# Convolution with a residual on one core: most of the weights' rows move from SyncE's queue to GpSimd's software queue

## The chip, the core and the metric

The kernel runs on one core of a Trainium2 chip. The metric is the device time of one execution in microseconds; lower is better. A core has five engines that work side by side, each with its own program: TensorE (PE, matrix products), VectorE (DVE), ScalarE (ACT), GpSimd (POOL) and SyncE (SP), which here only issues transfers. Transfers between the chip's memory (HBM) and the core's own memory (SBUF) are carried out by 16 DMA engines. A transfer can be issued by SyncE, or by GpSimd[...]. Engines wait for one another, and for transfers, through semaphores; a transfer adds 16 to its semaphore when it has landed.

## The reference

A 3x3 convolution with padding 1 over 16 images of 64 channels and 64x64 points, plus a residual, all in float32:

```python
batch, c_in, h, w, c_out, k = 16, 64, 64, 64, 64, 3
x_pad = np.pad(x, ((0, 0), (0, 0), (pad, pad), (pad, pad)), mode='constant')
output[b, co] += weight[co, ci, kh, kw] * x_pad[b, ci, kh:kh+h, kw:kw+w]   # summed over ci, kh, kw
return (output + residual).astype(np.float32)
```

x, the residual and the output are 16.8 MB each. The weights are 64 x 64 x 3 x 3 numbers, 147 KB.

## The kernel before

The images are taken in eight pairs; a pair fills the 128 partitions (2 images x 64 channels) with 4096 points each, 2 MB. The weights are read as 128 "half rows": for each output channel two rows of 32 input channels x 9 taps, 288 numbers or 1152 bytes.

All transfers go through SyncE's queue, in this order. The first pair's load is moved by a helper to the very front of the program, ahead of a barrier at which all engines meet at the start; everything after it is issued behind that barrier:

```python
    w_rows = weight.rearrange("co (h ci) kh kw -> (co h) (ci kh kw)", h=2)
    wraw = nc.alloc_sbuf_tensor("wraw", [128, 288], FP32)
    # ... cut
        for p in range(NPAIR):
            if p >= NXR:
                nc.sync.wait_ge(s_half, 2 * (p - NXR) + 3)      # a buffer of x is free again
            if p == 0:
                to_the_front(load_x(p))
                nc.sync.dma_start(out=wraw[:, :], in_=w_rows[:, :]).then_inc(s_w, 16)
            else:
                load_x(p)
            if p in (0, 1, 3, 5, 7):
                load_ro((p + 1) // 2)                            # residual, one or two pairs
        for k in range(NEARLY):                                  # three stores of two pairs
            nc.sync.wait_ge(s_add, 4 * k + 5)
            store(slice(2 * k, 2 * k + 2)).then_inc(s_out, 16)
    # ... cut; two stores of one pair follow at the end
```

GpSimd fills an identity matrix and zeroes some edges:

```python
        nc.gpsimd.memset(ident[:, :], 0.0).then_inc(s_id, 1)
        # ... cut: the diagonal, the edges of the four xp tiles, two blocks of wl
```

Before these lines GpSimd's program has four small memsets of constants, which stand ahead of the start-up barrier.

TensorE waits for the identity and the weights, transposes the weights in nine steps, and, once ScalarE and VectorE have copied them into bf16 blocks (wl), runs the convolution: 24 matrix products per image.

```python
        nc.tensor.wait_ge(s_id, NZERO)
        nc.tensor.wait_ge(s_w, 16)
        wraw3 = wraw.rearrange("p (ci t) -> p ci t", t=9)
        for t in range(9):
            i = nc.tensor.transpose(
                out=tp[0:32, t // 3, 128 * (t % 3) : 128 * (t % 3) + 128], in_=wraw3[:, :, t], identity=ident[:, :]
            )
```

ScalarE casts each image to bf16 (xp<-xr); VectorE adds TensorE's result to the residual in place (ro<-ps,ro), and ro is what is stored.

The helper that moves a transfer to the front takes the instruction out of the current block and puts it into the program's first block, ahead of the issuing engine's drain at the barrier:

```python
        at = next(
            i for i, e in enumerate(front) if e.engine == ins.engine and isinstance(e, mybir.InstDrain)
        )
        front.insert(at, copy.replace(ins, ...))
```

Of the kernel before, what the change touches and what calls it, by code (L numbers as in the profile page):

```python
# [15 lines left out]
def kernel(  # L16
# [7 lines left out]
    nc = tc.nc  # L24
# [20 lines left out]
    w_rows = weight.rearrange("co (h ci) kh kw -> (co h) (ci kh kw)", h=2)  # L45
# [9 lines left out]
    wraw = nc.alloc_sbuf_tensor("wraw", [128, 288], FP32)  # L55
# [1 line left out]
    ps = [psum.tile([128, NCHUNK, JC, W], FP32, name=f"ps{i}") for i in range(2)]  # L57

    sem = lambda name: tc.alloc_semaphore(name)
    s_w = sem("s_w")  # L60
    s_x = [sem(f"s_x{i}") for i in range(NXR)]
    s_r = [sem(f"s_r{i}") for i in range(2)]
    s_out = sem("s_out")
    s_id = sem("s_id")
    s_half = sem("s_half")
    s_pack = sem("s_pack")
    s_bank = sem("s_bank")
    s_conv = sem("s_conv")
    s_add = sem("s_add")

    def load_x(p):
        return nc.sync.dma_start(out=xr[p % NXR][:, :], in_=x_bc[128 * p : 128 * p + 128, :]).then_inc(s_x[p % NXR], 16)

    def load_ro(i):
        if i >= 2:
            nc.sync.wait_ge(s_r[i % 2], 16 * (i // 2))
        nc.sync.dma_start(out=ro[:, RES[i], :], in_=res_bc[:, RES[i], :]).then_inc(s_r[i % 2], 16)
# [24 lines left out]
    def to_the_front(dma):  # L102

        def fixed(ap):
            t = ap.bass_ap.tensor.name
            return mybir.PhysicalAccessPattern(
                ap=ap.ap, offset=ap.bass_ap.offset, dtype=ap.dtype, memref=t, memsetref=t + "_set", bass_ap=ap.bass_ap
            )  # L110

        front = nc.main_func.blocks[0].instructions
        here = nc.cur_bb.bb.instructions
        ins = here.pop()
        assert ins.name == dma.ins.name
        at = next(
            i for i, e in enumerate(front) if e.engine == ins.engine and isinstance(e, mybir.InstDrain)
        )
        front.insert(at, copy.replace(ins, ins=[fixed(a) for a in ins.ins], outs=[fixed(a) for a in ins.outs]))

# [4 lines left out]
    def weight_block(h, half, d, par, kh):  # L125

        at = 64 * half + 32 * h
        return dict(out=wl[at : at + 32, d, :, par, :], in_=tp[0:32, kh, 0:384].rearrange("p (kw co h) -> p kw co h", kw=3, h=2)[:, :, :, h])

    with tc.tile_critical(no_gpsimd_drain=True):  # L130

        for p in range(NPAIR):
            if p >= NXR:

                nc.sync.wait_ge(s_half, 2 * (p - NXR) + 3)
            if p == 0:
                to_the_front(load_x(p))
                nc.sync.dma_start(out=wraw[:, :], in_=w_rows[:, :]).then_inc(s_w, 16)
            else:
                load_x(p)  # L140
            if p in (0, 1, 3, 5, 7):
                load_ro((p + 1) // 2)
        for k in range(NEARLY):
            nc.sync.wait_ge(s_add, 4 * k + 5)
            store(slice(2 * k, 2 * k + 2)).then_inc(s_out, 16)


        nc.gpsimd.memset(ident[:, :], 0.0).then_inc(s_id, 1)  # L148
        nc.gpsimd.wait_ge(s_id, 1)
        nc.gpsimd.affine_select(  # L150
            out=ident[:, :],
            in_=ident[:, :],
# [14 lines left out]
        for n in range(B):  # L167
# [6 lines left out]
            i = nc.scalar.copy(out=t[64:128, 0:J, :], in_=x4[hp, :, 0, :])  # L174
# [4 lines left out]
            if n == 0:  # L179
                nc.scalar.wait_ge(s_id, NZERO + 1)  # L180
                for b in blocks[4:]:
                    for h in range(2):
                        i = nc.scalar.copy(**weight_block(h, *b))  # L183
# [4 lines left out]
        for k, b in enumerate(blocks[:4]):  # L188
            for h in range(2):
                i = nc.vector.tensor_copy(**weight_block(h, *b))  # L190
# [3 lines left out]
        for n in range(B):  # L194
# [4 lines left out]
            if im == 0:  # L199
                i = next(i for i, pairs in enumerate(RES) if p < pairs.stop)  # L200
                nc.vector.wait_ge(s_r[i % 2], 16 * (i // 2 + 1))
            for par in range(2):
                i = nc.vector.tensor_tensor(  # L203
                    out=o4[hp, :, par, :], in0=psj[64 * par : 64 * par + 64, :, :], in1=o4[hp, :, par, :], op=ADD
                )
# [4 lines left out]


        nc.tensor.wait_ge(s_id, NZERO)
        nc.tensor.wait_ge(s_w, 16)
        wraw3 = wraw.rearrange("p (ci t) -> p ci t", t=9)
        for t in range(9):
            i = nc.tensor.transpose(  # L216
                out=tp[0:32, t // 3, 128 * (t % 3) : 128 * (t % 3) + 128], in_=wraw3[:, :, t], identity=ident[:, :]
            )
# [23 lines left out]
        store(slice(p, p + 1))  # L242
    with tc.tile_critical(sync_engine=mybir.EngineType.Pool, no_gpsimd_drain=True):
        nc.gpsimd.wait_ge(s_out, 16 * NEARLY)
        tc.free_semaphores([s_w, *s_x, *s_r, s_out, s_id, s_half, s_pack, s_bank, s_conv, s_add])


# [28 lines left out]
```

## Time and profile before

| | before |
|---|---|
| device time, median of 3 (lowest to highest) | 122.76 us (122.69 to 122.91) |
| profiled execution: time, span | 122.68 us, 120.8 us |
| busy: PE, DVE, ACT, POOL | 87.9, 76.0, 63.1, 2.4 us |
| bytes moved, mean rate over the span | 50.48 MB, 418 GB/s |
| weights, from issue to landing | 7.1 us |
| first load of x, from issue to landing | 7.8 us |

The span runs from the first to the last instruction of the profiled execution, so it is shorter than the device time. A profile names a line of the kernel (L72), an engine, an operation and the tiles, output first. "SPq" stands for SyncE's sequencer, which issues transfers. A transfer's landing is counted from its issue and holds all its waiting behind others in the queue. The rates in the row of 40 slices are what all 16 DMA engines moved in each slice.

### The profile page before, as it was taken

What the parts mean: (1) busy time and instruction counts of PE and PEld (TensorE: products, weight loads), DVE (VectorE), ACT (ScalarE), POOL (GpSimd) and SP (SyncE); (2) the same over time, 40 slices, a digit from 0 to 9 for tenths busy, and PEclk for the clock granted to TensorE, in tenths of its full rate; (3) what the DMA queues carried; (4) which work ended last, traced back from release to release, by engine and by line L of the source; (5) the groups of instructions that cost most, each with busy time, mean ns of one, the idle gap of its engine ahead of it and who ended that gap; (6) DMA issues with size and microseconds to landing.
All of it is one profiled execution on the core that took longest, in us unless ns stands there. A gap on an engine that the chain in (4) does not pass through costs nothing.

```text
span 120.8 us, 734 instructions
## 1 busy us (share of the span) xinstructions
PE 87.9 (73%) x393; PEld 10.7 (9%) x105; DVE 76.0 (63%) x40; ACT 63.1 (52%) x37; POOL 2.4 (2%) x16
## 2 busy tenths in 40 slices
PE   0024499999999999999999999999999990000000
PEld 0011001101010011011111111011111100000000
DVE  0005400789898988989879898988989879500000
ACT  4049959948999923999960999883000000000000
POOL 5200000000000000000000000000000000000000
PEclk9999999999999999999999999999999999855555
DMA  7999999999999999999999999999999999999994
GB/s 168 428 428 428 428 428 434 428 434 434 428 434 434 434 428 434 434 434 434 434 434 423 423 428 434 423 412 434 434 434 434 423 434 434 434 428 434 434 434 174
DMA packets 3504, 50.48 MB, mean 418 GB/s; under 512 B 304, under 2 KB 432, under 8 KB 432
## 3 DMA queue, kind: packets, MB, share of 16 engines
q1 hardware_dynamic: 3504, 50.48, 98.5%
HBM read 33.70 MB, written 16.78 MB: 418 GB/s over the span
## 4 chain that ended last, share of the span: by engine, by line
PE 71%; DVEq 2%; DVE 2%; issue 0%
PE ps L87 53%; PE ps L86 18%; DVEq L130 2%; DVE ro L203 2%
## 5 line engine op out<-in xcount | busy, mean ns | idle before, releaser
L203 DVE TENSOR_TENSOR ro<-ps,ro 64x2048 f32<-64x2048 f32 x32 | 73.2, 2289 | 17.7 <-PE ps L87 17.2
L87 PE MATMUL ps<-xp,wl 128*128 128x504 bf16 (+1 forms) x288 | 80.0, 388 | 0.0
L86 PE MATMUL ps<-xp,wl 128*128 128x504 bf16 (+1 forms) x96 | 37.4, 389 | 3.4 <-PEq L224 3.4
L174 ACT CAST xp<-xr 64x2048 bf16<-64x2048 f32 x16 | 30.3, 1896 | 18.3 <-DMA xr<-in_x_dram 17.2
L178 ACT CAST xp<-xr 64x2048 bf16<-64x2048 f32 x16 | 30.4, 1897 | 0.4
L86 PEld LDWEIGHTS ps<-xp,wl 128*128 128x128 bf16 x96 | 9.5, 99 | 79.1 <-issue 79.1
L190 DVE CAST wl<-ps 32x192 bf16<-32x192 f32 x8 | 2.8, 348 | 10.6 <-PE ps L216 10.5
L216 PE MATMUL ps<-ident,wraw 128*32 128x128 f32 x9 | 2.1, 413 | 8.3 <-DMA wraw<-in_weight_dram 8.3
L216 PEld LDWEIGHTS ps<-ident,wraw 128*32 128x32 f32 x9 | 1.2, 137 | 8.7 <-issue 8.2
L174 ACT ACT_TABLE_LOAD x1 | 1.3, 1283 | 1.0 <-SPq L130 1.0
L183 ACT CAST wl<-ps 32x192 bf16<-32x192 f32 x4 | 1.2, 306 | 0.0
L162 POOL MEMSET xp<- 64x64 bf16 x4 | 0.6, 147 | 0.2
L161 POOL MEMSET xp<- 64x64 bf16 x4 | 0.6, 145 | 0.2
L150 POOL TENSOR_SCALAR_AFFINE_SELECT ident<-ident 128x128 f32<-128x128 f32 x1 | 0.3, 294 | 0.2 <-POOL ident L148 0.2
L164 POOL MEMSET wl<- 64x192 bf16 x1 | 0.3, 253 | 0.1
L163 POOL MEMSET wl<- 64x192 bf16 x1 | 0.3, 252 | 0.1
L148 POOL MEMSET ident<- 128x128 f32 x1 | 0.2, 205 | 0.6 <-SPq L130 0.6
L260 POOL MEMSET const-bfloat16-1.0<- 128x1 bf16 x1 | 0.1, 112 | 0.0
L260 POOL MEMSET const-uint8-127<- 128x1 uint8 x1 | 0.1, 112 | 0.0
L260 POOL MEMSET const-float32-0.0<- 128x1 f32 x1 | 0.1, 105 | 0.2 <-issue 0.2
L260 POOL MEMSET const-float32-1.0<- 128x1 f32 x1 | 0.1, 109 | 0.0
## 6 DMA issues: line engine op xcount, KB each, us to landing
xr<-in_x_dram SPq DMA_DIRECT2D x8, 2048.0 KB, 15.3
ro<-in_residual_dram SPq DMA_DIRECT2D x3, 4096.0 KB, 24.0
out_dram<-ro SPq DMA_DIRECT2D x3, 4096.0 KB, 33.2
ro<-in_residual_dram SPq DMA_DIRECT2D x2, 2048.0 KB, 15.9
out_dram<-ro SPq DMA_DIRECT2D x2, 2048.0 KB, 12.8
wraw<-in_weight_dram SPq DMA_DIRECT2D x1, 144.0 KB, 7.1
```

Of the source, the lines that this page charges most:

```text
L86: return e.matmul(out=out_, lhsT=lhsT, rhs=rhs, start=start, stop=stop, skip_group_check=True)
L87: return e.add_instruction(mybir.InstMatmult(name=nc.get_next_instruction_name(), engine=PE, ins=[e.lower_ap(rhs), e.lower_ap(lhsT)], outs ...
L130: with tc.tile_critical(no_gpsimd_drain=True):
L161: nc.gpsimd.memset(t[0:64, 0, :], 0.0).then_inc(s_id, 1)
L162: nc.gpsimd.memset(t[64:128, J, :], 0.0).then_inc(s_id, 1)
L174: i = nc.scalar.copy(out=t[64:128, 0:J, :], in_=x4[hp, :, 0, :])
L178: nc.scalar.copy(out=t[0:64, 1 : J + 1, :], in_=x4[hp, :, 1, :]).then_inc(s_pack, 1)
L183: i = nc.scalar.copy(**weight_block(h, *b))
L190: i = nc.vector.tensor_copy(**weight_block(h, *b))
L203: i = nc.vector.tensor_tensor(out=o4[hp, :, par, :], in0=psj[64 * par : 64 * par + 64, :, :], in1=o4[hp, :, par, :], op=ADD)
L216: i = nc.tensor.transpose(out=tp[0:32, t // 3, 128 * (t % 3) : 128 * (t % 3) + 128], in_=wraw3[:, :, t], identity=ident[:, :])
L260: nc = _bacc.Bacc("TRN2", target_bir_lowering=False, num_devices=1)
```

## The change

Of the weights' 128 half rows, the first 112 are now loaded by GpSimd's software queue. That transfer is put at the front of GpSimd's program, ahead of its constant memsets and so ahead of the start-up barrier, as the first load of x is on SyncE. The other 16 rows stay second on SyncE's queue. Each part has a semaphore of its own, and TensorE waits for both. The purpose is that most of the weights no longer stand behind the first load of x on one queue. The amount of data is the same; nothing else moves on TensorE, VectorE, ScalarE or SyncE.

```diff
-    s_w = sem("s_w")
+    s_w = [sem(f"s_w{i}") for i in range(2)]
...
+    def load_w(engine, rows, sem):
+        return engine.dma_start(out=wraw[rows, :], in_=w_rows[rows, :]).then_inc(sem, 16)
...
-            i for i, e in enumerate(front) if e.engine == ins.engine and isinstance(e, mybir.InstDrain)
+            i for i, e in enumerate(front) if e.engine == ins.engine and isinstance(e, (mybir.InstDrain, mybir.InstMemset))
...
-                nc.sync.dma_start(out=wraw[:, :], in_=w_rows[:, :]).then_inc(s_w, 16)
+                load_w(nc.sync, slice(112, 128), s_w[1])
...
+        to_the_front(load_w(nc.gpsimd, slice(0, 112), s_w[0]))
         nc.gpsimd.memset(ident[:, :], 0.0).then_inc(s_id, 1)
...
-        nc.tensor.wait_ge(s_w, 16)
+        for sem in s_w:
+            nc.tensor.wait_ge(sem, 16)
```

More of the change, by code (lines that the diff above doesn't have):

```diff
@@ L244 @@
         nc.gpsimd.wait_ge(s_out, 16 * NEARLY)
-        tc.free_semaphores([s_w, *s_x, *s_r, s_out, s_id, s_half, s_pack, s_bank, s_conv, s_add])
+        tc.free_semaphores([*s_w, *s_x, *s_r, s_out, s_id, s_half, s_pack, s_bank, s_conv, s_add])
 _INS = ['x', 'weight', 'residual']
```

## The prediction

> **What bounds the kernel now.** I read the chain that ended last first, since it names what the program seems to wait for, and then the page's row of slices and its queue table to see whether that chain is really the limit.
>
> ```profile
> span 120.8 us, 734 instructions
> PE 71%; DVEq 2%; DVE 2%; issue 0%
> PE ps L87 53%; PE ps L86 18%; DVEq L130 2%; DVE ro L203 2%
> ...
> GB/s 168 428 428 428 428 428 434 428 434 434 428 434 434 434 428 434 434 434 434 434 434 423 423 428 434 423 412 434 434 434 434 423 434 434 434 428 434 434 434 174
> q1 hardware_dynamic: 3504, 50.48, 98.5%
> HBM read 33.70 MB, written 16.78 MB: 418 GB/s over the span
> ```
>
> The chain names TensorE, but it covers only about 75% of the span; the rest of the time is after its last instruction. The row of slices says why: each slice is 120.8/40 = 3.02 us, and in 38 of 40 the transfers run at 412 to 434 GB/s. The one hardware queue fills 98.5% of sixteen engines' time. So the transfers are the bound. Only the first and last slices fall short, and the time can change only by the bytes in the queue, by the ramp at the start, or by a gap that opens in the queue.
>
> The windows view splits the start and the end (columns: stretch, length, then busy us of PE, PEld, DVE, ACT and POOL with counts, clock, mean DMA share, GB/s):
>
> ```profile
> 0.00:1.00 1.00, 0.00 (x0) 0.00 (x0) 0.00 (x0) 0.04 (x1) 0.22 (x5) 1.00 0.00 0
> 1.00:3.00 2.00, 0.00 (x0) 0.00 (x0) 0.00 (x0) 1.24 (x1) 1.39 (x9) 1.00 1.10 254
> 3.00:6.00 3.00, 0.00 (x0) 0.00 (x0) 0.00 (x0) 0.00 (x0) 0.78 (x4) 1.00 1.01 431
> 6.00:8.00 2.00, 0.00 (x0) 0.00 (x0) 0.00 (x0) 0.21 (x1) 0.00 (x0) 1.00 0.98 401
> ...
> 119.60:120.80 1.20, 0.00 (x0) 0.00 (x0) 0.00 (x0) 0.00 (x0) 0.00 (x0) 0.50 0.00 0
> ```
>
> Nothing moves for 1.0 us after the first issue. For the next 2 us the engines count as busy (share 1.10) but move only 254 GB/s: that is latency, not throughput. In the trace's packet records the first 16 KB packet of each engine takes 0.72 to 2.03 us, and a later one 0.611 us. The ramp therefore loses (431 - 254) x 2.0 us = 354 KB, or 354/431 = 0.82 us of full-rate work. The small dip to 401 GB/s at 6 to 8 us is where the weights' 128 packets of 1152 bytes pass: in the records each takes 51 ns and the next on the same engine starts 47 ns after it, so eight rows per engine take 8 x 47 = 0.38 us.
>
> The timeline shows who waits for those weights:
>
> ```profile
> 0.00 0.38 SPq L72 DMA_DIRECT2D xr<-in_x_dram  x1
> 1.00 0.33 SPq L138 DMA_DIRECT2D wraw<-in_weight_dram  x1
> 7.79 1.90 ACT L174 CAST xp<-xr 64x2048 bf16<-64x2048 f32 x1 [5.55 <-DMA xr<-in_x_dram]
> 8.27 2.08 PE L216 MATMUL ps<-ident,wraw 128*32 128x128 f32 x9 [8.27 <-DMA wraw<-in_weight_dram]
> 13.78 0.59 PE L86 MATMUL ps<-xp,wl 128*128 128x512 bf16 x1 [3.44 <-PEq L224]
> 99.67 4.61 DVE L203 TENSOR_TENSOR ro<-ps,ro 64x2048 f32<-64x2048 f32 x2 [0.58 <-PE ps L87]
> 104.58 0.98 SPq L80 DMA_DIRECT2D out_dram<-ro  x2
> ```
>
> The weights are second on SyncE's queue, so they land just behind the first image pair, and TensorE transposes them from 8.27 us. Its convolution then runs almost unbroken from 13.78 to 99.67 us. The last two stores are issued at 104.58 us, yet the packet records show the store ahead of them finishing at 109.9 us and the last one at 119.6 us. Allowing the 1.0 us from issue to first packet, compute could be about 109.4 - 104.6 - 1.0 = 3.8 us later before the queue ran dry (109.4 is when the first engine finishes that earlier store). An earlier convolution gains nothing.
>
> [...] The trace has 1.007 us from the issue to the first packet on SyncE's queue[...] and the software one is unseen. [...]
>
> **The change part by part.**
> Removed from SyncE's queue: 112 of 128 rows, 112 x 1152 = 129 KB. By the packet records that is seven packets per engine, 7 x 47 = 0.33 us; by bytes at 431 GB/s it is 0.30 us. This comes straight off the path, since SyncE's queue is the chain that really ends last.
>
> Added on GpSimd's queue: the same seven packets per engine and one completion packet (9 ns in the records for this kind). What they cost depends on when they run. GpSimd's first instruction in the trace starts at 0.23 us, the issue now stands ahead of it[...]. That falls in the ramp, which has 0.82 us of unused room against the 0.30 us needed. If they fit, the cost is only about 0.01 us; if they come after 3 us, they take 0.33 us from the first pair at full rate and the gain is nil.
>
> Moved on GpSimd: its four constant memsets, the start-up barrier behind them, the identity and the zero fills go back by however long GpSimd takes[...]. SyncE passes that barrier at about 1.0 us now. [...] the queue holds the first pair's packets until the first engine completes them at 6.44 us. So the barrier can slip by about 6.4 - 1.0 - 1.0 = 4.4 us before an engine idles. The fills end at 3.94 us and the transposes need them at about 8 us, again 4 us of room.
>
> Kept: 16 rows, one packet per engine, still behind the first pair. TensorE waits for both parts, so its start stays tied to that pair's end; it moves by at most 0.3 us either way, into the 3.8 us of slack, and counts for nothing. One more semaphore wait is too small to see.
>
> Sum: between -0.33 + 0.01 = -0.32 us (all rows in the ramp) and +0.01 us (none). I weight the full case above the empty one, since the issue is at the very front, and take -0.26 us: 122.76 - 0.26 = 122.50 us.
>
> **The rivals.**
> First, no gain because the ramp is not free. If the slow first packets are a shortage at the memory, and not a latency of each queue, added packets stretch them. For it: total rate in the ramp is low on all engines at once (254 GB/s). Against: the packets there look like waiting, with all sixteen engines showing long first packets and then 0.611 us at once. The time would stay at 122.7 to 122.9 us.
>
> Second, the software queue costs more than it saves: [...] some extra work at the program's start or end that comes with using it. The wait for the weights then moves from SyncE's queue to GpSimd's. As long as they land before about 11.5 us (3.8 us of slack past 7.8 us) only the lost packet time counts, and the result is 122.8 to 123.2 us.
>
> Third, GpSimd is held long enough to hold up the start-up barrier past its 4.4 us. [...] Against it: the issue was put at the front by design, and the memsets around it are ordinary GpSimd work that runs at once.
>
> A gain beyond 0.4 us has no source: even a perfect ramp, with the weights free, would leave 50.3 MB at about 431 GB/s on the queue.
>
> **Range and chances.** About half the weight is on 122.4 to 122.6 us, a quarter on no change near 122.8, the rest above. That gives 122.2 to 123.2 us for 8 times in 10. Two per cent is 2.46 us, so faster by that would need 120.3 us, which no step here can give: 0.01. Slower by that needs 125.2 us, the hard end of the third rival: 0.03. Within 2%: 0.96.
>
> **What would show it.** Right: a software queue with about 0.13 MB in the queue table; its 1152-byte packets starting before 3 us; the first slice's GB/s above 168; no dip at 6 to 8 us; first pair landing at about the same time; the whole run of transfers about 0.3 us shorter; the stores' backlog at the end still there. Wrong: the software rows starting after 3 us or landing after 8 us; SyncE's second issue later than about 5.4 us with a hole in the early slices; a GpSimd DMA taking several us; or a span that grows at the end, with the transfers over but the program not.

## The result, and the profile after

The changed kernel takes 126.25 us (median of 6 runs, 125.99 to 126.69), the kernel before 122.81 us in the same comparison: ratio 1.0283, 95% interval 1.0263 to 1.0302. It is 3.4 us slower. I had predicted 122.5 us, with a range of 122.2 to 123.2.

The page of the changed kernel, the lines that answer to those of before (its row of 40 slices is now 3.13 us to the slice):

```profile
span 125.4 us, 735 instructions
...
GB/s 172 421 116 199 429 434 434 423 439 429 429 439 434 423 439 423 434 439 429 429 423 439 429 434 434 434 402 434 423 418 439 434 439 439 423 418 434 434 434 125
...
q1 hardware_dynamic: 3392, 50.35, 95.4%
q0 software_dynamic: 48, 0.13, 0.3%
```

The software queue is there with its 0.13 MB, and takes 0.3% of the engines' time. The third and fourth slices have fallen to 116 and 199 GB/s, where before every slice but the first and last had over 400. So the queue ran dry for a time between 6 and 12 us. The windows view places it (same columns as in the prediction; the last is GB/s):

```profile
3.00:6.00 3.00, 0.00 (x0) 0.00 (x0) 0.00 (x0) 0.00 (x0) 0.00 (x0) 1.00 0.95 392
6.00:8.00 2.00, 0.00 (x0) 0.00 (x0) 0.00 (x0) 0.00 (x0) 0.00 (x0) 1.00 0.69 255
8.00:10.00 2.00, 0.00 (x0) 0.00 (x0) 0.00 (x0) 1.10 (x1) 0.71 (x4) 1.00 0.03 5
10.00:12.00 2.00, 0.07 (x1) 0.07 (x2) 0.00 (x0) 1.99 (x2) 1.44 (x9) 1.00 0.85 192
12.00:14.00 2.00, 2.00 (x9) 1.12 (x9) 0.00 (x0) 1.98 (x2) 0.00 (x0) 1.00 1.01 434
```

Between 8 and 10 us almost nothing moves, and from 10 to 12 us there is a second ramp at 192 GB/s. Over the first 14 us the engines average 249 GB/s against 372 in the kernel before; (372 - 249) x 14 us = 1.72 MB, and at 429 GB/s that is 4.0 us. The profiled span grew by 4.5 us (from 120.85 to 125.40 us in the trace), so nearly all of it is lost here; behind 14 us the mean rate is 426 against 429 GB/s. The timeline of the changed kernel shows who held the queue:

```profile
0.00 0.38 SPq L75 DMA_DIRECT2D xr<-in_x_dram  x1
0.75 0.65 POOL L72 DMA_DIRECT2D wraw<-in_weight_dram  x1 [0.75 <-issue]
1.44 0.10 POOL L265 MEMSET const-float32-0.0<- 128x1 f32 x1
1.54 0.10 POOL L265 MEMSET const-uint8-127<- 128x1 uint8 x1
8.90 1.28 ACT L178 ACT_TABLE_LOAD   x1 [8.90 <-SPq L133]
8.94 0.35 SPq L72 DMA_DIRECT2D wraw<-in_weight_dram  x1
8.94 0.20 POOL L152 MEMSET ident<- 128x128 f32 x1 [7.30 <-SPq L133]
17.44 0.58 PE L89 MATMUL ps<-xp,wl 128*128 128x512 bf16 x1 [3.40 <-PEq L229]
```

GpSimd's issue takes 0.65 us and its constant memsets are over at 1.64 us. Then no engine does any work until 8.90 us, when ScalarE, SyncE and GpSimd all start at once: the start-up barrier has opened, 7.9 us later than before. SyncE's second issue moves from 1.00 to 8.94 us. The transfers' landings say what came just ahead of that (KB, then us from issue to landing):

```profile
wraw<-in_weight_dram POOLq DMA_DIRECT2D x1, 126.0 KB, 7.7
wraw<-in_weight_dram SPq DMA_DIRECT2D x1, 18.0 KB, 1.7
```

The software rows were issued at 0.75 us and landed 7.7 us later, at 8.40 us; 0.5 us after that SyncE issued again. In the trace's packet records the first software packet starts only at 4.61 us and the last one ends at 7.92 us.

In the profiled runs device time minus span was 122.68 - 120.85 = 1.8 us before and is 126.69 - 125.40 = 1.3 us here, so the time grew 0.5 us less than the span. (126.69 us is the slowest of the six runs; hence 4.0 us in the profiled runs and 3.4 us in the medians.)

### The profile page after: what moved, and what is told of

It is laid out like the page before. It is cut to its first block, busy times and chain, and to the rows that moved or that the text cites. A ratio compares the mean times of both kernels' runs of the same rounds, so it can differ in the third digit from the quotient of the medians.

```text
span 125.4 us, 735 instructions
## 1 busy us (share of the span) xinstructions
PE 87.4 (70%) x393; PEld 10.7 (9%) x105; DVE 76.0 (61%) x40; ACT 63.2 (50%) x37; POOL 3.0 (2%) x17
## 5 line engine op out<-in xcount | busy, mean ns | idle before, releaser
L178 ACT CAST xp<-xr 64x2048 bf16<-64x2048 f32 x16 | 30.3, 1896 | 13.7 <-DMA xr<-in_x_dram 13.1
L72 POOL DMA_DIRECT2D wraw<-in_weight_dram x1 | 0.6, 646 | 0.7 <-issue 0.7
## 6 DMA issues: line engine op xcount, KB each, us to landing
out_dram<-ro SPq DMA_DIRECT2D x2, 2048.0 KB, 13.7
```

Of the source, the lines that this page charges most:

```text
L72: return engine.dma_start(out=wraw[rows, :], in_=w_rows[rows, :]).then_inc(sem, 16)
```

## The experiments

Theory A: GpSimd's program has a drain ahead of the start-up barrier, and this drain does not end until the software transfer issued ahead of it has landed; the barrier opens half a microsecond later, and by then SyncE's queue is empty. Theory B: GpSimd itself is held for a fixed time by the issue, and everything it does next waits. Theory C: the second queue slows the DMA engines, whatever the barrier does.

**The same issue, behind the drain.** Only the place in GpSimd's program differs from the changed kernel: behind the drain, still ahead of its wait at the barrier.

```diff
+        if ins.engine == mybir.EngineType.Pool:
+            at = 1 + next(i for i, e in enumerate(front) if e.engine == ins.engine and isinstance(e, mybir.InstDrain))
```

> The same software load of 112 rows, issued by GpSimd behind its drain instead of ahead of it, still before the start-up barrier is released. Theory A (GpSimd's drain ahead of the barrier does not end until the software transfer has landed, here 8.4 us, and the barrier opens some 0.5 us later): the barrier opens at about 1.0 us as in the kernel before, SyncE's second issue is at about 1.0 us, no hole in the transfers, time 122.5 to 123.0 us. Theory B (GpSimd itself is held[...], so everything it does next waits): either the barrier still opens at about 8.9 us and the time is about 126.2, or it opens early and GpSimd's identity memset starts only at about 8 us. Theory C (a second, software-fed queue slows the DMA engines): the time stays near 126 us although the barrier opens early.

Measured: 123.33 us (before in the same comparison: 122.89); ratio 1.0035, interval 1.0021 to 1.0049. Its timeline:

```profile
1.07 0.65 POOL L72 DMA_DIRECT2D wraw<-in_weight_dram  x1 [0.62 <-POOLq L267]
1.47 0.35 SPq L72 DMA_DIRECT2D wraw<-in_weight_dram  x1
1.72 0.22 POOL L154 MEMSET ident<- 128x128 f32 x1
9.19 2.08 PE L223 MATMUL ps<-ident,wraw 128*32 128x128 f32 x9 [9.19 <-DMA wraw<-in_weight_dram]
```

SyncE issues again at 1.47 us, and GpSimd fills its identity at 1.72 us, right after its issue ends, while the software rows are still 3 us from their first packet. So GpSimd was not held past its issue: theory B falls. Moving one issue past one drain takes back 3.0 of the 3.4 us. The time is still 0.44 us over before, 0.33 us above what A expected; that rest is taken up below.

**The same rows by ScalarE's hardware queue, at the front.**

```diff
-        to_the_front(load_w(nc.gpsimd, slice(0, 112), s_w[0]))
+        to_the_front(load_w(nc.scalar, slice(0, 112), s_w[0]))
```

> The same 112 rows at the front, issued by ScalarE on its hardware queue instead of GpSimd's software queue. Theory A (a software transfer under GpSimd's drain): with no software transfer the barrier opens at about 1.0 us; no hole; and if a second queue is served during the ramp the rows start before 2.5 us and the time is 122.4 to 122.7 us (the gain of up to 0.32 us that the prediction hoped for), or 122.7 to 122.9 us if the ramp is not free. If every drain waits for its engine's transfer, the barrier opens only when these rows land, at about 3 to 4 us, which is still early enough to leave no hole. Theory C for any second queue: near 126 us.

Measured: 122.93 us against 122.89; ratio 1.0007, interval 0.9996 to 1.0019. The barrier opens at about 1.1 us although the rows land at 8.4 us, so ScalarE's drain did not wait here for the transfer on its hardware queue (it lasts 0.15 us in the trace). A second queue costs nothing here, but gains nothing either. Windows of this kernel:

```profile
1.00:3.00 2.00, 0.00 (x0) 0.00 (x0) 0.00 (x0) 1.28 (x1) 1.32 (x8) 1.00 1.00 247
3.00:6.00 3.00, 0.00 (x0) 0.00 (x0) 0.00 (x0) 0.00 (x0) 0.84 (x5) 1.00 1.05 443
```

The ramp is as slow as before (247 against 254 GB/s): the rows' first packet starts at 2.98 us, when the ramp is about over, although the issue was at 0.12 us. From then on the rows take turns with x: sixteen of them, as many as there are DMA engines, start about every 0.67 us until 7.64 us, which is the time of one 16 KB packet of x (0.61 us) and one row (0.05 us).

**More work on SyncE's queue ahead of the held barrier.** The software load stays ahead of the drain; the second pair of x is issued ahead of the barrier too, and the 16 rows come by ScalarE's queue.

```diff
-                load_w(nc.sync, slice(112, 128), s_w[1])
+                load_w(nc.scalar, slice(112, 128), s_w[1])
+            elif p == 1:
+                to_the_front(load_x(p))
```

> The software load stays ahead of GpSimd's drain as in the changed kernel, but SyncE issues the second pair of x ahead of the barrier too, so that its queue holds 2 x 4.9 us of work; the 16 rows come by ScalarE's queue behind the barrier. Theory A and B (the loss is SyncE's queue running dry while the barrier is held): barrier still at about 8.5 to 9.5 us, no hole in the transfers until 12 us, time 122.5 to 123.2 us. Theory C (the software queue's own cost to the DMA engines): still 125 us or more.

Measured: 123.94 us (122.69 to 124.39) against 122.89; ratio 1.0069, interval 1.0048 to 1.0091. The barrier is held as in the changed kernel (SyncE's next issue at 8.86 us), yet no slice of its page but the first and last is under 363 GB/s: with more in the queue there is no hole, and most of the loss is gone. The median missed the expectation on the high side. In its packet records most 16 KB packets of the first two residual loads, from 12 to 24 us, take 0.700 us instead of 0.611 (218 of 256 to within 0.01 us); the x loads before and after them do not. That is 2 x 2.1 MB at 379 (14 to 23 us) instead of 431 GB/s, 1.3 us. The same stretch shows in the profiled run of the kernel with the issue behind the drain, for one residual load (0.7 us; this was its slowest run, 124.18 us). What causes it was not settled.

**Only 16 rows by the software queue.**

```diff
-                load_w(nc.sync, slice(112, 128), s_w[1])
+                load_w(nc.sync, slice(16, 128), s_w[1])
-        to_the_front(load_w(nc.gpsimd, slice(0, 112), s_w[0]))
+        to_the_front(load_w(nc.gpsimd, slice(0, 16), s_w[0]))
```

> Only 16 rows by the software queue, ahead of the drain as in the changed kernel; the other 112 second on SyncE's queue. Theory A with a fixed start-up of the software queue (its first packet came 3.9 us after its issue with 112 rows): the rows land at 5.5 to 7.5 us, the barrier opens 0.4 to 0.5 us after that, the hole is smaller, time 123.5 to 125.5 us. If the hold grows with the rows: landing near 2 us, no hole, 122.7 to 123.0 us. Theory B[...]: barrier at about 8.9 us as with 112 rows, time 126 us or more.

Measured: 125.23 us against 122.89; ratio 1.0184, interval 1.0169 to 1.0199. The rows land 6.1 us after their issue and SyncE issues again at 7.33 us: a seventh of the rows, and still four fifths of the hold (6.3 of 7.9 us). The first software packet starts at 4.99 us, as late as with 112 rows. Most of the delay is in when the software queue is first served, less in how much it carries: from the first packet to the landing it is 1.8 us with 16 rows and 3.8 us with 112.

**The software rows alone.** The first load of x is issued behind the barrier too.

```diff
-                to_the_front(load_x(p))
+                load_x(p)
```

> The changed kernel with the first load of x issued behind the barrier too, so that the software rows are alone on the DMA engines. Theory A (GpSimd's drain waits for the landing): the rows land earlier than the 8.4 us after the start that they took beside x, and the barrier opens 0.4 to 0.5 us after that landing, whenever it is; the first software packet tells the software queue's own start-up: if about 3.9 us after the issue again, it is the queue's, if about 1 to 2 us, it was the waiting behind x. Theory B (a fixed hold of GpSimd): the barrier still opens 8.1 us after the software issue. The time itself is expected at 126 to 129 us, since x starts only behind the barrier.

Measured: 125.61 us, one run, just under the expected 126 to 129 us. Timeline and landing of the rows:

```profile
0.75 0.65 POOL L72 DMA_DIRECT2D wraw<-in_weight_dram  x1 [0.75 <-issue]
3.70 0.38 SPq L75 DMA_DIRECT2D xr<-in_x_dram  x1
```

```profile
wraw<-in_weight_dram POOLq DMA_DIRECT2D x1, 126.0 KB, 2.4
```

The same transfer now lands at 3.17 us, and the barrier opens with it. Its first packet comes at 2.10 us, 1.35 us after the issue; beside the load of x it came 3.86 us after it. So alone the software queue takes 1.35 us to start, and the other 2.5 us came only with x's packets in flight; how they come about is not shown. The trace holds GpSimd's drain itself, as a record of its sequencer (here the kernel before, the changed kernel and this one; shortest, median and longest in ns, then first and last start in us):

```profile
L260 POOLq DRAIN  x1: 196/196/196, 0.3 to 0.3; - x1
L265 POOLq DRAIN  x1: 7658/7658/7658, 0.8 to 0.8; - x1
L265 POOLq DRAIN  x1: 2423/2423/2423, 0.8 to 0.8; - x1
```

The four kernels with a software issue ahead of the drain, from their records:

| kernel | rows landed at | drain ended at | SyncE's next issue |
|---|---|---|---|
| changed kernel | 8.40 us | 8.48 us | 8.94 us |
| more ahead | 8.33 us | 8.41 us | 8.86 us |
| 16 rows | 6.80 us | 6.88 us | 7.33 us |
| software alone | 3.17 us | 3.25 us | 3.70 us |

The landing varies by 5.2 us, and in all four the drain ends 0.08 us after it and SyncE issues 0.53 us after it: the barrier follows the landing, as theory A has it.

**The hold without the software queue.** The kernel before, with the barrier held by two long GpSimd memsets into buffers that are loaded later.

```diff
+        for i in (1, 2):
+            to_the_front(nc.gpsimd.memset(xr[i][:, :], 0.0))
         nc.gpsimd.memset(ident[:, :], 0.0).then_inc(s_id, 1)
```

> The kernel before, all weights on SyncE's queue, no software transfer; only the barrier is held, by two GpSimd memsets of 128 x 4096 ahead of the drain (estimate from the 128 x 128 memset's 205 ns against 105 to 112 ns for one element: 3.0 us each). Theory A (the cost is the held barrier and the queue running dry): the barrier opens at about 7 us, the transfers stop at about 7.5 to 8 us and start again 1.0 us after SyncE's second issue, and the time is 125.0 to 126.2 us. Theory C (the software queue itself is what costs): 122.7 to 123.2 us.

Measured: 126.12 us against 122.96; ratio 1.0250, interval 1.0227 to 1.0274. Timeline:

```profile
0.36 6.97 POOL L149 MEMSET xr<- 128x4096 f32 x2
7.79 1.28 ACT L176 ACT_TABLE_LOAD   x1 [7.79 <-SPq L130]
7.83 0.33 SPq L138 DMA_DIRECT2D wraw<-in_weight_dram  x1
```

A barrier that opens at 7.8 us costs 3.2 us with no software transfer in the program, as A expected. SyncE issues 1.1 us earlier than in the changed kernel, and the profiled span is 1.2 us shorter (124.2 against 125.4 us); in device time the 0.5 us noted with the result bring the two close together. The loss of the changed kernel needs nothing but the hold; theory C falls for its main part.

**The software rows behind the barrier**, as GpSimd's last instruction.

```diff
-        to_the_front(load_w(nc.gpsimd, slice(0, 112), s_w[0]))
...
         nc.gpsimd.memset(wl[64:128, 1, :, 0, :], 0.0).then_inc(s_id, 1)
+        load_w(nc.gpsimd, slice(0, 112), s_w[0])
```

> The software load of 112 rows as GpSimd's last instruction, behind the barrier and its fills, at about 4 us. Theory A: barrier at about 1.0 us, no hole, rows 3.9 us after their issue, landing at 9 to 12 us, the convolution 1.5 to 4 us later than before, inside or at the edge of the 3.8 us of slack; time 122.6 to 123.4 us. Theory C: 125 us or more.

Measured: 123.27 us against 122.96; ratio 1.0026, interval 1.0014 to 1.0038. Issued at 3.89 us, the rows land 6.8 us later, and the time is inside what A expected. The first packet comes 3.8 us after the issue here too, long after the ramp, so the wait does not belong to the ramp. Windows around the rows' packets (7.7 to 10.3 us in the records):

```profile
7.00:8.00 1.00, 0.00 (x0) 0.00 (x0) 0.00 (x0) 0.00 (x0) 0.00 (x0) 1.00 0.90 360
8.00:10.00 2.00, 0.00 (x0) 0.00 (x0) 0.00 (x0) 1.86 (x1) 0.00 (x0) 1.00 1.00 340
```

While software packets pass, the engines are busy but move 340 to 360 GB/s in all, the rows included. The lost bytes, (431 - 360) x 1 + (431 - 340) x 2 = 253 KB or 0.6 us, exceed the 0.14 us of the dip that the rows made on SyncE's queue in the kernel before; by 14 us the packet records have this kernel 0.19 MB, or 0.4 us, behind that one. So the software queue has a price of its own, a few tenths of a microsecond, which also lies in the right place for the rest of the kernel with the issue behind the drain (380 GB/s between 5 and 8 us). What the engines do in that time was not separated.

**The rows first on SyncE's own queue**, ahead of the first load of x.

```diff
-        to_the_front(load_w(nc.gpsimd, slice(0, 112), s_w[0]))
...
+                to_the_front(load_w(nc.sync, slice(0, 112), s_w[0]))
                 to_the_front(load_x(p))
```

> The 112 rows at the very front of SyncE's own queue, ahead of the first load of x, the other 16 second behind the barrier; no second queue. If the ramp's 0.8 us is a latency that a queue's next packets share, the rows' packets fill it and the time falls by up to 0.3 us: 122.4 to 122.7 us. If the ramp begins anew with the first load of x (issued 0.4 us later), nothing is gained or up to 0.4 us is lost: 122.8 to 123.3 us.

Measured: 123.24 us (122.87 to 124.04) against 122.96; ratio 1.0036, interval 1.0020 to 1.0052. The rows' packets do start in the ramp, at 1.01 us, and x's issue slips to 0.45 us. Windows:

```profile
1.00:3.00 2.00, 0.00 (x0) 0.00 (x0) 0.00 (x0) 1.28 (x1) 1.07 (x6) 1.00 1.12 245
3.00:6.00 3.00, 0.00 (x0) 0.00 (x0) 0.00 (x0) 0.00 (x0) 1.09 (x7) 1.00 0.96 410
```

The total in the ramp does not rise, and is lower just after it (410 against 431 GB/s). But two things changed: SyncE issued x 0.45 us after the rows, so x's first packet slipped too, from 1.01 to 1.51 us, and its last packets end 0.42 us later (7.48 against 7.06 us, mean of the engines). By 14 us the kernel is 45 KB, or 0.1 us, behind the kernel before. That is about what a start 0.4 us later costs, less the 0.33 us of rows that no longer follow x; whether the ramp had room for rows without a later x is not told apart. The 22 runs lie in two groups, 11 at 122.87 to 123.10 (the profiled run among them) and 11 at 123.39 to 124.04; no trace of the upper group was kept, so the gap between them is not explained. No version here beats the kernel before.

## Why the prediction was wrong, step by step

**The bound was read rightly.** The transfers set the time before and after, and the slack of the convolution was real: it starts 3.66 us later (17.44 against 13.78 us), while the last stores, issued from 108.16 us on, still stand in a queue that ends at 124.2 us. One reading was off: the chain that names TensorE runs from 13.7 to 104.3 us, so of the quarter of the span that it leaves out, 13.7 us lie ahead of it and 16.5 us after it, not all after it.

**The step that failed** is "Moved on GpSimd": "the identity and the zero fills go back by however long GpSimd takes". GpSimd's issue was done in 0.65 us. What holds the barrier is the drain ahead of it: it lasts 7.66 us instead of 0.20, until the rows have landed, 7.7 us after the issue. I had worked out that the barrier could slip by 4.4 us before an engine idles; it slipped by 7.9 us. In the packet records x's last packets end at 7.60 us and the next ones start at 9.98 us (means of the engines), a hole of 2.4 us. The restart loses another 1.4 us: from 9.98 to 14 us 1.12 MB move, which at 431 GB/s is 2.6 us of work. The two are 3.8 of the 4.0 us found in the first 14 us. I had the budget and the wrong event to hold against it. The kernel with the issue behind the drain, against the changed one, shows it, and so does the barrier held by memsets alone.

**Where the rows run** failed too. I placed the rows in the ramp; that was my estimate, since no trace of the kernel before has a second queue or a software queue. Alone, the first packet came 1.35 us after the issue; beside the load of x it came 3.86 us after it, and GpSimd issued at 0.75 us, not at the 0.23 us that I had counted from. I took a place on a queue of their own for prompt service. The rows do take turns with x, as ScalarE's rows show once they have begun (sixteen about every 0.67 us); but a second queue's first packet waited until 2.98 us (ScalarE's, issued at 0.12 us) or 4.6 to 5.1 us (GpSimd's, issued ahead of the barrier at 0.74 to 1.07 us). Nor did the rows go as seven packets per engine: the software queue carried them as two, of 4608 and 3456 bytes, four rows and three. Whether a second issuing engine gains anything could not be read from the trace of the kernel before, where SyncE issues everything; in ScalarE's run, at a ratio of 1.0007, it gained nothing.

**The gain of 0.32 us** appeared in no run. Whether the ramp is free, which the first rival denies, was not decided: ScalarE's and GpSimd's rows came behind it, and the rows that SyncE put into it made x start later.

**The rivals.** The third named the right place, the barrier held past its budget, and the sign of a hole in the early slices. It gave the wrong cause, GpSimd itself held: GpSimd's next instruction ran 0.04 us after its DMA instruction ended. I gave it too little weight, 0.03 for a time of 125.2 us or more. Of my signs of being wrong, the rows starting after 3 us (4.61), landing after 8 us (8.40), and a late second issue (8.94) with a hole all came; a long GpSimd DMA did not. The second, the software queue's own cost, is real at 0.3 to 0.4 us by the two kernels that issue it without a long hold.

## What to carry to other kernels

Before moving a GpSimd transfer ahead of a barrier, look for a drain between the two: here the drain lasted until the software transfer had landed (7.66 us instead of 0.20), while ScalarE's drain did not wait for its hardware queue (the barrier opened at about 1.1 us, the rows landed at 8.4 us). When engines are held at the start, ask how many microseconds of transfers are already queued: with one load of x in the queue a barrier at 8.9 us left a hole of 2.4 us, with two it left none. That number is the budget, and the event to hold against it was, for the software transfer here, the landing and not the issue. Where the transfers are the bound, do not count on moving a small load: in the four runs that moved these rows without a long hold of the barrier (ratios 1.0007 to 1.0036) nothing was gained.

## What the runs showed of the hardware that was not expected

GpSimd's drain lasted until a software transfer issued ahead of it had landed, to within 0.08 us in four kernels. A second queue's first packet came late beside a running load of 16 KB packets: GpSimd's 112 rows took 7.7 us from issue to landing beside it, 2.4 us alone. With the software DMA as GpSimd's first instruction ahead of the constants, device time minus span is 1.3 us instead of 1.8 us, in all four such kernels; where those 0.5 us go was not found. And residual loads ran at about 380 instead of 431 GB/s in two of the profiled runs, with packets of about 0.700 us, while the x loads before and after them were at full rate.
